# Latent attention in ascending tiles, with keys and queries made in one stream between the attention's half steps

## The chip, the cores and the metric

The kernel runs on one core of one Trainium2 chip. The metric is the device time of one execution in microseconds. Five engines work side by side, each with an in-order instruction queue: TensorE (PE, matrix products and transposes, results in PSUM), VectorE (DVE), ScalarE (ACT), GpSimd (POOL) and SyncE (SP, which here only starts DMA transfers).

## The reference

A trunk of two layers on a sequence of 1024 tokens with 1024 features, all float32. A layer normalises its input, projects it once, and feeds four branches of 256 features each: A (gated causal depthwise convolution of 31 taps, LayerNorm, swish, pointwise product), B (HGRN2, a gated linear recurrence), C (Mamba-2 SSD in chunks) and D (multi-head latent attention). The outputs are gated, concatenated, projected with `w_out`, normalised and added to the input. What changes is mostly branch D:

```python
def mla_branch(cq, ckv, k_rope, gate, positions, qa_g, qb_w, kva_g, kvb_w):
    q = (rms_norm(cq, qa_g) @ qb_w).reshape(bsz, s, D_HEADS, D_NOPE + D_ROPE)
    q = jnp.concatenate([q[..., :D_NOPE], apply_rotary(q[..., D_NOPE:], positions)], axis=-1)
    kv = (rms_norm(ckv, kva_g) @ kvb_w).reshape(bsz, s, D_HEADS, D_NOPE + D_VDIM)
    ...
    mask = key_chunk[None, :] <= q_chunk[:, None]
    p = jax.nn.softmax(jnp.where(mask, sc, MASK_VALUE), axis=-1)
    return (p @ v) * jax.nn.silu(gate)
```

It has 4 heads, a query rank of 256, a key/value rank of 128, 64 plain and 32 rotary features a head and 64 value features. The mask is causal by chunks of 64 tokens, so a tile of 128 queries reads the keys of its own tile and of all tiles before it.

## The kernel before, in words

Work goes by tiles of 128 tokens (`NT` = 8) and, where features lie in the partitions, by halves of 512 tokens. The normalised input stands transposed in SBUF as two pools of 32 KB a partition, a high and a low part (`hT`), because large projections are made of three products of split operands. The output weights, split in the same way by `th_w` (L939), take the place of `hT`: they can be written when the last projection has read it.

Each branch is a set of Python generators ("threads"): `th_conv` (L470, the 31 taps on DVE, 30 multiply-adds of 128x512 for each of 2 feature halves and 2 sequence halves), `th_atail` (L482, LayerNorm, swish and product of branch A for the two sequence halves), `th_b`, `th_x` and `th_c` (L715, the scan of branch C, tile by tile), `gate_f` (gates of A and D), `th_d` (L788, the latents of D), `th_q` (L852, queries of D), `th_att` (L883, attention), `th_w` and `th_o` (L987, the first output tile). `PLAN` (L44) gives each thread a start, an end and a total of work units, and `weave` (L259) always runs the thread whose position in that plan is earliest. So the plan sets the order in which instructions are written down; a scheduler then orders them for each engine by when they could start, with the written order as priority, and gives out the buffers.

In `th_d`, for each tile of `ORDER` (L37, 7 down to 0): 24 products into `psd` (L206 to L208), copies `cn` and `krd` out of it, the squares and `rstd_p` on POOL (L143, L144), the query scale `rq` on DVE, transposes of `cn` (L823), copies `ckT` and `cqT`; then `pk` (L832), the scaled keys `kk` and values `vD`, the rotary part of the key (five DVE operations), transposes of the keys (L845) and copies `kT`. Keys of all tiles stay in `kT`, query latents in `cqT`. `th_q` makes the queries of a tile from `cqT`: `pq` (L857), scaled copy, four rotary operations on DVE, transposes `ptq` (L870), copy `qTt`. Rows 96 to 99 of `kT` and `qTt` hold mask factors that DMAs on POOL's queue bring.

`th_att` goes through `ORDER` too. For each pair of heads (`m`) it makes the scores of two heads (`psc`, L900), their negated maximum (`nm`, L903, DVE), the exponentials with their sums (`pe`, L905, ACT), yields, then transposes the exponentials (`ptp`, L914), copies them (`pT`, three of four on DVE) and multiplies with the values (`poD`, L918). A tile ends with the reciprocal of the sums spread over 256 columns on DVE (`rsD`, L925), its two transposes (`prsD`, L928) and two multiplications with the gate `gD`. Attention of tile 7 comes first and needs the keys of all tiles, so attention begins when `th_d` has ended. `th_o` multiplies the first output tile (`ORDER[0]`) by the output weights; the other tiles follow in the same order, and so does the next layer.

PSUM has two tiles of two banks (`big`: `psd`, `pk`, `psc`, `pz` and others) and two single banks for each of two groups (`sm`): one group holds `ptp`, `ptA` and others, the other `ptx`, `pcb`, `pyC` of branch C and `pq`, `ptq`, `poD` of D. In SBUF the groups of buffers that matter are `t1k` (six of 256 columns: `xdt`, `xsd`, `btk`, `yo` of branch C, `gD`, `rsD`, `yD` of D) and `blk` (19 of 512 columns).

Of the kernel before, what the change touches and what calls it, by code (L numbers as in the profile page):

```python
# [15 lines left out]
ALU = mybir.AluOpType  # L16
# [8 lines left out]
NT1, NT15, NT2 = 6, 2, 4  # L25
# [11 lines left out]
ORDER = list(range(NT))[::-1]  # L37
# [35 lines left out]
    "gd1": (261.8, 280.6, 21),  # L73
    "x1": (212.9, 255.7, 61.5),
    "at1": (278.6, 342, 22),
    "c1": (275.5, 340.6, 48.2),
    "d1": (266.1, 351.4, 72),
    "q1": (335.5, 349.5, 2),
    "o1": (479.4, 508.2, 8.2),
    "att1": (347.1, 481.6, 144.8),  # L80
# [16 lines left out]
def trunk_kernel(ctx, tc, x, pos, pre_g, post_g, wd, wv, w256, wo, cols, rows, pw, qb, kvb,  # L97
# [161 lines left out]
    def weave(threads, until):  # L259

        while threads:
            t = min(threads, key=Thread.pos)
            if t.pos() > until:
                return
# [11 lines left out]
    for l in range(L):  # L276
# [193 lines left out]
        def th_conv():  # L470
            for m in range(2):
                w = [col[:, C_DWW + m * 31 + k:C_DWW + m * 31 + k + 1] for k in range(31)]
                for h in range(2):
# [8 lines left out]
        def th_atail():  # L482
            for g in range(2):
# [231 lines left out]
        def th_c():  # L715
            hst = small(256, "hst", 1)
            G.memset(hst, 0.0)
            for g4 in range(2):
                gt = get_gate(2, g4)
                ms = small(8, "msc", 2)  # L720
                for j in range(4):
# [51 lines left out]
                    jk = br.tile([P, 256], BF16, tag="jk", name="jkC", bufs=1)  # L773
# [11 lines left out]
        kT, vD, cqT = {}, {}, {}  # L785
        rq = small(NT, "rq", 1)

        def th_d():  # L788
# [7 lines left out]
            for i in ORDER:  # L796
                g = i // 4
                if (0, g) not in kT:
                    for h in range(4):
                        kT[h, g] = blk("kT", parts=100)  # L800

                        nc.gpsimd.dma_start(out=kT[h, g][96:100, :], in_=amask[0])
                    for c in range(2):
                        cqT[c, g] = blk("cqT")
# [7 lines left out]
                ms = small(2, "msd", 3)  # L812
# [3 lines left out]
                krd = small(32, "krd", 2, (P, 2, 16))  # L816
                copy("krd", krd.rearrange("p a j -> p (a j)"), ps[:, 384:416])
                A.activation(jd[:, 0:256], cn[:, 0:256], AF.Square, scale=1.0 / 16, accum_out=ms[:, 0:1])
                A.activation(jd[:, 256:384], cn[:, 256:384], AF.Square, scale=128.0 ** -0.5, accum_out=ms[:, 1:2])
                rstd_p(ms, ms)  # L820
                V.tensor_scalar(rq[:, i:i + 1], ms[:, 0:1], SCALE, None, op0=ALU.mult)
# [15 lines left out]
                k1, k2 = small(32, "kr1", 2, (P, 2, 16)), small(32, "kr2", 2, (P, 2, 16))  # L837
                V.tensor_tensor(k1, krd, cosT[:, i], op=ALU.mult)
                for a in range(2):
                    V.tensor_tensor(k2[:, a, :], krd[:, 1 - a, :], sinT[:, i, a, :], op=ALU.mult)  # L840
                V.tensor_tensor(k1, k1, k2, op=ALU.add)
                V.tensor_copy(kk[:, :, 64:96],
                              k1.rearrange("p a j -> p (a j)").unsqueeze(1).to_broadcast([P, 4, 32]))
# [4 lines left out]
                yield 3  # L848

        qTs = {}  # L850

        def th_q():  # L852
            for i in ORDER:
                csl = slice((i % 4) * P, (i % 4 + 1) * P)
                pq = sm("pq")
                for c in range(2):
                    T.matmul(pq[:, 0:384], cqT[c, i // 4][:, csl], qbt[:, c, :], start=(c == 0), stop=(c == 1))  # L857
                qk = tmp(384, "qk", (P, 4, 96))
                scaled("qk", qk.rearrange("p h d -> p (h d)"), pq[:, 0:384], rq[:, i:i + 1])
                t1, t2 = small(128, "rt1", 1, (P, 4, 2, 16)), small(128, "rt2", 1, (P, 4, 2, 16))  # L860
                qr = qk[:, :, 64:96].rearrange("p h (a j) -> p h a j", a=2)
                V.tensor_tensor(t1, qr, cosT[:, i].unsqueeze(1).to_broadcast([P, 4, 2, 16]), op=ALU.mult)
                for a in range(2):
                    V.tensor_tensor(t2[:, :, a, :], qr[:, :, 1 - a, :],
                                    sinT[:, i, a, :].unsqueeze(1).to_broadcast([P, 4, 16]), op=ALU.mult)
                V.tensor_tensor(qk[:, :, 64:96], t1.rearrange("p h a j -> p h (a j)"),
                                t2.rearrange("p h a j -> p h (a j)"), op=ALU.add)
# [3 lines left out]
                qTt = br.tile([100, 4, P], F32, tag="qTt", name="qTt", bufs=2)  # L871
                nc.gpsimd.dma_start(out=qTt[96:100, :, :].rearrange("p h t -> p (h t)"), in_=amask[1 + i % 4])
                copy("qTt", qTt[0:96, :, :].rearrange("p h t -> p (h t)"), ptq[0:96, :])
                qTs[i] = qTt
                yield 1

        q_steps = th_q()

        def th_q0():
            yield next(q_steps)  # L880
            yield next(q_steps)

        def th_att():  # L883
            for i in ORDER:
# [273 lines left out]
```

## Time and profile before

| | us |
|---|---|
| median of 3 runs (1263.44 to 1266.04) | 1265.05 |
| the profiled execution | 1263.62 |
| its span | 1261.8 |
| PE busy | 1195.5 |
| DVE busy | 876.9 |
| ACT busy | 445.3 |
| POOL busy | 184.2 |

The profile is of one execution; its time is 1.8 us more than the span from the first to the last instruction. Busy time of PE is time in which at least one product is under way by the profiler's model; time of an engine that is not busy is idle. Layer 0 takes about the first 640 us, layer 1 the rest. In each layer the convolution ends some 350 us (in layer 1 at about 968) into the span, the latents of D some 90 us later, and attention about 545 (1162); the output projection follows.

### The profile page before, as it was taken

The page shows a single profiled execution, that of the slowest core. Times are in us where ns is not written, and L with a number is a line of the kernel's source. Part 1 is how long each engine was busy: PE and PEld are TensorE (multiplying, and loading weights), DVE is VectorE, ACT ScalarE, POOL GpSimd, SP SyncE. Part 2 cuts the span into 40 slices and gives each one's busy share as a digit, 9 for nine tenths or more (in the row PEclk, how much of TensorE's full clock was granted, in tenths as well). Part 3 has the DMA queues.
Part 4 walks back from the last instruction along what each step waited for, and adds up shares of the span by engine and source line. Part 5 has one row for each costly group of instructions (what it writes and reads, how often), then busy time and mean ns, then how long its engine had stood idle before and what let it go on. Part 6 is the DMA issues. An engine that isn't in the chain of part 4 may idle for free.

```text
span 1261.8 us, 17893 instructions
## 1 busy us (share of the span) xinstructions
PE 1195.5 (95%) x6902; PEld 985.5 (78%) x6902; DVE 876.9 (69%) x1687; ACT 445.3 (35%) x1028; POOL 184.2 (15%) x290
## 2 busy tenths in 40 slices
PE   5999999899989989999999999998999998999997
PEld 5988998888878746678888889887888776566886
DVE  5564699999876386745453839999997763867232
ACT  5412222222374364434332222221225644644211
POOL 2100020111033111111020001211012322112000
PEclk9999999999999999999999999999999899999999
DMA  7102122111151040144321111211013311202531
GB/s 274 34 34 68 43 76 85 67 46 51 55 165 60 22 152 24 56 154 137 114 97 60 41 50 59 84 63 64 34 62 124 105 35 55 93 18 68 188 128 72
DMA packets 38660, 101.47 MB, mean 80 GB/s; under 512 B 5440, under 2 KB 13808, under 8 KB 38576
## 3 DMA queue, kind: packets, MB, share of 16 engines
q1 hardware_dynamic: 22848, 51.42, 12.0%
q0 software_dynamic: 14864, 46.04, 11.0%
q10 hardware_dynamic: 864, 2.88, 0.6%
q8 instruction: 54, 0.88, 0.3%
q14 instruction: 30, 0.25, 0.1%
HBM read 75.37 MB, written 25.20 MB: 80 GB/s over the span
## 4 chain that ended last, share of the span: by engine, by line
PE 40%; DVE 11%; ACT 2%; issue 1%; DMA 1%; POOL 0%; DVEq 0%; ACTq 0%
PE pz L982 11%; DVE ca L478 2%; PE psx L217 2%; PE psx L223 2%; PE psx L220 2%; DVE amat L639 2%; PE psc L900 1%; DVE qz L632 1%; PE psA L217 1%; PE psA L220 1%; PE psA L223 1%; PE poD L918 1%; PE ptp L914 1%; PE psd L206 1%; PE psd L208 1%
## 5 line engine op out<-in xcount | busy, mean ns | idle before, releaser
L478 DVE SCALAR_TENSOR_TENSOR ca<-hpad,col,ca 128x512 f32<-128x512 f32 x240 | 179.8, 751 | 3.6
L173 DVE TENSOR_TENSOR wl<-raw,wh 128x1024 fp32r<-128x1024 f32 (+2 forms) x56 | 66.9, 1194 | 81.0 <-ACT wh L157 80.9
L157 ACT CAST wh<-raw 128x1024 fp32r<-128x1024 f32 (+2 forms) x56 | 57.5, 1028 | 154.0 <-PE psA L220 33.7
L982 PE MATMUL pz<-woh,yh 128*128 128x512 f32 x240 | 77.8, 403 | 0.2 <-ACT yh L157 0.2
L982 PE MATMUL pz<-woh,yl 128*128 128x512 f32 x240 | 75.6, 396 | 0.0
L982 PE MATMUL pz<-wol,yh 128*128 128x512 f32 x240 | 75.4, 396 | 0.0
L206 PE MATMUL psg<-wh,hh 128*128 128x256 f32 x256 | 74.4, 291 | 1.1 <-DVE amat L608 1.1
L622 PE MATMUL plB<-qz,krb 128*128 128x128 f32 x448 | 63.6, 287 | 10.8 <-DVE krb L633 10.6
L900 PE MATMUL psc<-kT,qTt 96*128 96x512 f32 (+4 forms) x192 | 72.6, 501 | 1.2 <-ACT pe L905 1.1
L208 PE MATMUL psg<-wh,hl 128*128 128x256 f32 x256 | 73.1, 286 | 0.0
L207 PE MATMUL psg<-wl,hh 128*128 128x256 f32 x256 | 72.7, 284 | 0.0
L905 ACT ACTIVATE pe<-psc,nm 128x1024 f32<-128x1024 f32 (+7 forms) x64 | 47.3, 739 | 63.5 <-DVE nm L903 63.0
L622 PEld LDWEIGHTS plB<-qz,krb 128*128 128x128 f32 x448 | 57.0, 197 | 13.6 <-issue 7.1
L217 PE MATMUL psx<-hh,wh 128*128 128x512 f32 x192 | 62.8, 404 | 0.0
L223 PE MATMUL psx<-hh,wl 128*128 128x512 f32 x192 | 62.0, 399 | 0.0
L220 PE MATMUL psx<-hl,wh 128*128 128x512 f32 x192 | 61.2, 400 | 0.0
L173 DVE TENSOR_TENSOR yl<-yt,yh 128x512 fp32r<-128x512 f32 x16 | 11.0, 690 | 65.2 <-ACT yh L157 65.2
L982 PEld LDWEIGHTS pz<-woh,yl 128*128 128x128 f32 x240 | 45.3, 189 | 10.5 <-issue 0.2
L982 PEld LDWEIGHTS pz<-wol,yh 128*128 128x128 f32 x240 | 45.3, 189 | 10.5
L903 DVE TENSOR_REDUCE nm<-psc 128x1 f32<-128x1024 f32 (+7 forms) x64 | 47.1, 744 | 9.0 <-PE psc L900 9.0
L914 PE MATMUL ptp<-idn,pe 128*128 128x128 f32 x288 | 46.8, 282 | 6.0 <-ACT pe L905 5.8
L157 DVE COPY pT<-ptp 128x512 f32<-128x512 f32 (+3 forms) x72 | 38.0, 546 | 20.5 <-PE ptp L914 20.4
(331 smaller groups left out, 3076.0 us busy)
## 6 DMA issues: line engine op xcount, KB each, us to landing
raw<-in_w_dram SPq DMA_DIRECT2D x44, 512.0 KB, 3.5
rawo<-in_wo_dram SPq DMA_DIRECT2D x16, 512.0 KB, 4.3
gsp<-gt POOLq DMA_DIRECT2D x16, 256.0 KB, 2.6
gl<-gsp POOLq DMA_DIRECT2D x8, 512.0 KB, 5.5
gspF<-gtA POOLq DMA_DIRECT2D x16, 256.0 KB, 2.3
ysp<-gl POOLq DMA_DIRECT2D x8, 512.0 KB, 3.4
lm<-acsp POOLq DMA_DIRECT2D x16, 256.0 KB, 4.1
yt<-ysp SPq DMA_DIRECT2D x16, 256.0 KB, 3.4
```

Source lines behind the costliest of these rows:

```text
L157: (V.tensor_copy if name in ONV else A.copy)(out_, in_)
L173: V.tensor_tensor(lo, src, hi.bitcast(F32), op=ALU.subtract)
L206: T.matmul(ps[:, :n], a, hs[k], start=(k == 0), stop=False)
L207: T.matmul(ps[:, :n], a, ls[k], start=False, stop=False)
L208: T.matmul(ps[:, :n], b, hs[k], start=False, stop=(k == KD - 1))
L217: T.matmul(ps[:, h * 512:(h + 1) * 512], w, hh[:, k, h * 512:(h + 1) * 512], start=(k == 0), stop=False)
L220: T.matmul(ps[:, h * 512:(h + 1) * 512], w, hl[:, k, h * 512:(h + 1) * 512], start=False, stop=False)
L223: T.matmul(ps[:, h * 512:(h + 1) * 512], wl, hh[:, k, h * 512:(h + 1) * 512], start=False, stop=(k == KD - 1))
L478: V.scalar_tensor_tensor(t, hp[:, k:k + 512], w[k], t, op0=ALU.mult, op1=ALU.add)
L622: T.matmul(pl[:, o0:o0 + P].rearrange("p (r b u) -> p r b u", r=2, u=u), k_[:, t_ * P:(t_ + 1) * P], z[:, :, t_ * P:(t_ + 1) * P].rearrang ...
L900: T.matmul(psc[:, c0:c1_], qTt[0:k_, h, :], kT[h, c0 // 512][0:k_, 0:c1_ - c0], start=True, stop=True)
L982: T.matmul(pz[n], a[:, k, :], w[:, k, n * 512:(n + 1) * 512], start=(k == 0 and a is yh and w is wh), stop=(k == KD - 1 and a is yl))
```

## The change

`ORDER` is ascending. `th_d` and `th_q` become one generator, `th_kq`, that makes keys, values and queries of one tile in four steps; `th_att` first runs it for two tiles (`AHEAD`), and then takes one step of it after each of the four half steps of an attention tile, so that tile i+2 is made during tile i and the last one during tile 5. The query latent is no longer stored for all tiles (`cqT`), and the rotary part of key and queries of a tile is made together (five heads, five DVE operations). The query scale moves to POOL. For tiles 0 to 3 the scores of two heads share one PSUM tile and one maximum. The reciprocal is taken of the four sums, and POOL spreads it over 256 columns; its transposes go into the upper half of the bank of `poD`. The masks and the gate of D are loaded on SP's queue; `gD` has one buffer of its own, and `t1k` has five. The convolution goes by sequence half, the two halves of branch A's tail are threads of their own (the first planned at 236 instead of 296), and the gate of D is planned about 10 units earlier. The place of `hT` is given to the output weights when `th_kq` has written down the last tile's projection.

```diff
-NT1, NT15, NT2 = 6, 2, 4
+NT1, NT15, NT2 = 5, 2, 4
-ORDER = list(range(NT))[::-1]
+ORDER = list(range(NT))
+AHEAD = 2
-    "gd0": (278.8, 298.3, 21),
+    "gd0": (268, 287, 21),
-    "at0": (296.3, 363.8, 22),
+    "at00": (236, 262, 11),
+    "at10": (302, 340, 11),
-    "d0": (283.6, 373.2, 72),
-    "q0": (357.3, 375.6, 2),
-    "att0": (347.7, 481.2, 144.8),
+    "att0": (288, 481.2, 217.6),
...
-        while threads:
+        while threads and not until():
...
         def th_conv():
-            for m in range(2):
-                for h in range(2):
+            for h in range(2):
+                for m in range(2):
...
-        def th_atail():
-            for g in range(2):
+        def th_atail(g):
...
+        def th_kq():
...
-                        nc.gpsimd.dma_start(out=kT[h, g][96:100, :], in_=amask[0])
-                    for c in range(2):
-                        cqT[c, g] = blk("cqT")
+                        nc.sync.dma_start(out=kT[h, g][96:100, :], in_=amask[0])
...
                 proj_tok(hT, hs, ls, i, ND, ps)
+                made.append(i)
...
+                rp = tmp(160, "rp", (P, 5, 2, 16))
+                copy("krd", rp[:, 4, :, :].rearrange("p a j -> p (a j)"), ps[:, 384:416])
...
-                V.tensor_scalar(rq[:, i:i + 1], ms[:, 0:1], SCALE, None, op0=ALU.mult)
+                G.tensor_scalar(ms[:, 2:3], ms[:, 0:1], SCALE, None, op0=ALU.mult)
+                yield 2.25
...
-                for c in range(2):
-                    copy(f"cqT{c}", cqT[c, g][:, csl], pt[:, c * P:(c + 1) * P])
-                yield 6
+                cqt = tmp(256, "cqt")
+                copy("cqt", cqt, pt[:, 0:256])
+                yield 2.25
                 pk_ = big("pk")
                 T.matmul(pk, ckT, kvt, start=True, stop=True)
+                pq = sm("pq")
+                for c in range(2):
+                    T.matmul(pq[:, 0:384], cqt[:, c * P:(c + 1) * P], qbt[:, c, :], start=(c == 0), stop=(c == 1))
...
+                scaled("qk", rp[:, 0:4, :, :].rearrange("p h a j -> p h (a j)"), pqv[:, :, 64:96], ms[:, 2:3])
+                scaled("qk", qk[:, :, 0:64], pqv[:, :, 0:64], ms[:, 2:3])
+                V.tensor_tensor(t1, rp, cosT[:, i].unsqueeze(1).to_broadcast([P, 5, 2, 16]), op=ALU.mult)
...
+                yield 2.25
                 for h in range(4):
                     T.transpose(ptk[0:96, h * P:(h + 1) * P], kk[:, h, :], idn)
...
+                qTt = br.tile([100, 4, P], F32, tag="qTt", name="qTt", bufs=AHEAD + 1)
+                nc.sync.dma_start(out=qTt[96:100, :, :].rearrange("p h t -> p (h t)"), in_=amask[1 + i % 4])
...
         def th_att():
+            kq = th_kq()
+            for _ in range(4 * AHEAD):
+                yield next(kq)
             for i in ORDER:
...
-                po = sm("poD")[:, 0:256]
+                pob = sm("poD")
+                po, prs = pob[:, 0:256], pob[:, 256:512]
-                gt = tmp(256, "gD", (P, 2, P))
-                nc.gpsimd.dma_start(out=gt, in_=feat(gspF, 1, i * P, (i + 1) * P))
+                gt = small(256, "gD", 1, (P, 2, P))
+                nc.sync.dma_start(out=gt, in_=feat(gspF, 1, i * P, (i + 1) * P))
...
                     yield i + 1
+                    w = next(kq, None)
+                    if w is not None:
+                        yield w
...
+                V.reciprocal(sume, sume)
                 rs = tmp(256, "rsD", (P, 4, 64))
-                V.reciprocal(rs, sume.unsqueeze(2).to_broadcast([P, 4, 64]))
-                prs = sm("prsD")[:, 0:256]
+                G.tensor_copy(rs, sume.unsqueeze(2).to_broadcast([P, 4, 64]))
...
-        weave(ths, plan("d")[1] + 0.5)
+        weave(ths, lambda: len(made) == NT)
         hpool.release()
```

## Rows read from the trace of the kernel before

**Rows 1.** the page, part 1, the whole span: busy us (share), instructions

```profile
PE 1195.5 (95%) x6902; PEld 985.5 (78%) x6902; DVE 876.9 (69%) x1687; ACT 445.3 (35%) x1028; POOL 184.2 (15%) x290
```

**Rows 2.** busy by stretch: us, PE, PEld, DVE, ACT, POOL busy (instructions), granted clock

```profile
140.00:350.00 210.00, 205.08 (x1277) 181.04 (x1277) 200.14 (x354) 51.19 (x90) 31.05 (x44) 0.98 0.19 63
350.00:444.00 94.00, 86.19 (x504) 72.52 (x502) 56.88 (x191) 50.28 (x165) 24.48 (x41) 1.00 0.24 79
444.00:457.00 13.00, 8.10 (x24) 4.14 (x24) 9.98 (x18) 9.14 (x22) 5.15 (x5) 0.87 0.56 177
457.00:480.00 23.00, 21.92 (x142) 13.63 (x141) 19.09 (x25) 15.35 (x24) 2.38 (x5) 1.00 0.34 116
480.00:533.00 53.00, 51.52 (x393) 35.37 (x392) 38.39 (x77) 22.49 (x55) 9.31 (x14) 1.00 0.09 28
533.00:545.00 12.00, 9.77 (x64) 7.03 (x63) 9.98 (x21) 5.28 (x16) 2.23 (x4) 0.86 0.39 116
760.00:968.00 208.00, 201.09 (x1257) 176.44 (x1257) 196.31 (x341) 50.18 (x88) 30.21 (x42) 0.99 0.18 63
968.00:1064.00 96.00, 89.11 (x504) 75.45 (x503) 56.22 (x185) 49.99 (x165) 24.17 (x40) 0.96 0.24 78
1064.00:1081.00 17.00, 11.34 (x37) 5.41 (x36) 12.71 (x26) 12.99 (x28) 5.15 (x5) 0.90 0.46 154
1081.00:1150.00 69.00, 67.32 (x499) 45.39 (x499) 52.30 (x92) 32.55 (x67) 9.71 (x15) 1.00 0.12 37
1150.00:1162.00 12.00, 10.21 (x80) 7.03 (x75) 9.66 (x24) 6.72 (x23) 2.86 (x4) 1.00 0.38 118
```

**Rows 3.** timeline of PE, 444 to 480: start, length, line, operation, idle before

```profile
445.69 1.12 PE L832 MATMUL pk<-kvt,ckT 128*128 128x512 f32 x2 [1.67 <-DVE ckT L157]
449.13 0.80 PE L845 MATMUL pk<-idn,kk 128*96 128x128 f32 x4 [2.32 <-ACT vD L163]
...
450.58 4.75 PE L900 MATMUL psc<-kT,qTt 96*128 96x512 f32 x8
...
465.17 1.67 PE L900 MATMUL psc<-kT,qTt 96*128 96x512 f32 x4
```

**Rows 4.** groups on DVE by shape, 340 to 560: busy us, mean ns, idle

```profile
L925 DVE RECIPROCAL rsD<-sume 128x256 f32<-128x256 f32 x8 | 13.9, 1742 | 0.0
...
L491 DVE BATCH_NORM_STATS2 stA<-ptA 128x6 f32<-128x256 f32 x8 | 3.4, 423 | 0.0
...
L513 DVE SCALAR_TENSOR_TENSOR glA<-pyA,col,glA 128x512 f32<-128x512 f32 x4 | 3.0, 748 | 0.7 <-PE pyA L512 0.7
...
L864 DVE TENSOR_TENSOR rt<-qk,sinT 128x64 f32<-128x64 f32 x16 | 2.9, 217 | 0.0
...
L497 DVE TENSOR_SCALAR hnA<-hnA,mvA 128x256 f32<-128x256 f32 x8 | 2.7, 405 | 0.5 <-POOL mvA L144 0.5
```

**Rows 5.** waits of PE, whole span: total us, times, longest

```profile
PE prsD L928 <- DVE rsD L925: 1.7, 2, 1.2
```

**Rows 6.** groups on POOL by shape, whole span

```profile
L647 POOL TENSOR_TENSOR qp<-qz 128x512 f32<-128x512 f32 x8 | 12.3, 1542 | 21.6 <-DVE qz L632 21.6
...
L891 POOL DMA_DIRECT2D gD<-gspF x16 | 11.5, 721 | 2.0 <-issue 2.0
```

**Rows 7.** timeline of POOL, 445 to 450 us

```profile
445.59 1.83 POOL L143 TENSOR_TENSOR msd<-msd,eps 128x2 f32<-128x2 f32 x1 [10.04 <-ACT jd L819]
...
448.19 0.19 POOL L143 TENSOR_TENSOR msc<-msc,eps 128x8 f32<-128x8 f32 x1
```

**Rows 8.** timeline of DVE, 444 to 449 us

```profile
445.55 1.21 DVE L173 TENSOR_TENSOR wol<-rawo,woh 128x1024 fp32r<-128x1024 f32 x1
```

**Rows 9.** waits of SP's queue, whole span: total us, times, longest

```profile
SPq L943 <- DVE ckT L157: 174.3, 2, 88.2
```

**Rows 10.** timeline of PE, line 733 (first step of a branch C tile)

```profile
382.01 0.60 PE L733 MATMUL ptx<-idn,xbc 128*128 128x128 f32 x4
...
412.87 0.60 PE L733 MATMUL ptx<-idn,xbc 128*128 128x128 f32 x4
```

More of the change, by code (lines that the diff above doesn't have):

```diff
@@ L470, in th_conv @@
         def th_conv():
-            for m in range(2):
-                w = [col[:, C_DWW + m * 31 + k:C_DWW + m * 31 + k + 1] for k in range(31)]
-                for h in range(2):
+            for h in range(2):
+                for m in range(2):
+                    w = [col[:, C_DWW + m * 31 + k:C_DWW + m * 31 + k + 1] for k in range(31)]
                     hp = hpads[m, h]
@@ L772, in th_c @@
                     V.tensor_tensor(gt[:, j, :], xsf, gt[:, j, :], op=ALU.mult)
-                    jk = br.tile([P, 256], BF16, tag="jk", name="jkC", bufs=1)
+                    jk = br.tile([P, 384], BF16, tag="jd", name="jkC", bufs=1)
                     for g in range(2):
@@ L782, in th_c @@
                 yield 0.1
-        kT, vD, cqT = {}, {}, {}
-        rq = small(NT, "rq", 1)
-        def th_d():
+        kT, vD, qTs = {}, {}, {}
+        made = []
+        def th_kq():
             nc.gpsimd.dma_start(out=qbt, in_=qb[l])
@@ L811, in th_d @@
                 proj_tok(hT, hs, ls, i, ND, ps)
-                ms = small(2, "msd", 3)
+                made.append(i)
+                ms = small(3, "msd", 3)
                 cn = tmp(384, "cn")
@@ L847, in th_d @@
                     copy(f"kT{h}", kT[h, g][0:96, csl], ptk[0:96, h * P:(h + 1) * P])
[L848 to L867, printed above, removed]
                 ptq = sm("ptq")
@@ L893, in th_att @@
                     pes = []
-                    for r in range(2):
-                        h = 2 * m + r
-                        psc = big("psc")
-                        for c0 in range(0, n, 512):
-                            c1_ = min(n, c0 + 512)
-                            k_ = 100 if c1_ == n else 96
-                            T.matmul(psc[:, c0:c1_], qTt[0:k_, h, :], kT[h, c0 // 512][0:k_, 0:c1_ - c0],
-                                     start=True, stop=True)
-                        nm = small(1, "nm", 3)
-                        V.tensor_reduce(nm, psc[:, 0:n], AX.X, ALU.max, negate=True)
-                        pe = k4("pe")
-                        A.activation(pe[:, 0:n], psc[:, 0:n], AF.Exp, bias=nm, accum_out=sume[:, h:h + 1])
-                        pes.append(pe)
+                    nm = small(2, "nm", 3)
@@ new lines, in th_att @@
+                    if i < 4:
+                        psc = big("psc")
+                        pe = k4("pe", (P, 2, 512))
+                        for r in range(2):
+                            T.matmul(psc[:, r * 512:r * 512 + n], qTt[:, 2 * m + r, :], kT[2 * m + r, 0][:, 0:n],
+                                     start=True, stop=True)
+                        pv = psc.rearrange("p (r k) -> p r k", r=2)[:, :, 0:n]
+                        V.tensor_reduce(nm, pv, AX.X, ALU.max, negate=True)
+                        scs = [psc[:, r * 512:r * 512 + n] for r in range(2)]
+                        pes = [pe[:, r, 0:n] for r in range(2)]
+                    else:
+                        scs = []
+                        for r in range(2):
+                            psc = big("psc")
+                            for c0 in range(0, n, 512):
+                                c1_ = min(n, c0 + 512)
+                                k_ = 100 if c1_ == n else 96
+                                T.matmul(psc[:, c0:c1_], qTt[0:k_, 2 * m + r, :], kT[2 * m + r, c0 // 512][0:k_, 0:c1_ - c0],
+                                         start=True, stop=True)
+                            V.tensor_reduce(nm[:, r:r + 1], psc[:, 0:n], AX.X, ALU.max, negate=True)
+                            scs.append(psc[:, 0:n])
+                            pes.append(k4("pe")[:, 0:n])
@@ L920, in th_att @@
                                  for j in range(j0, j1) for r in (1, 0))
-                    if m == 1:
-                        next(q_steps, None)
                     yield i + 1
+                    w = next(kq, None)
+                    if w is not None:
+                        yield w
+                V.reciprocal(sume, sume)
                 rs = tmp(256, "rsD", (P, 4, 64))
-                V.reciprocal(rs, sume.unsqueeze(2).to_broadcast([P, 4, 64]))
-                prs = sm("prsD")[:, 0:256]
+                G.tensor_copy(rs, sume.unsqueeze(2).to_broadcast([P, 4, 64]))
                 for m in range(2):
@@ L1007, in trunk_kernel @@
         wo_t["l"] = wpool.tile([P, KD, D], F32R, name=f"wol{l}")
-        ths += [Thread(th_att(), *plan("att")), Thread(th_w(), *plan("w")), Thread(th_o(), *plan("o"))]
-        weave(ths, 1e9)
+        ths += [Thread(th_w(), *plan("w")), Thread(th_o(), *plan("o"))]
+        weave(ths, lambda: False)
         br.release()
```

45 lines of the change are left out of this document (19 added, 26 removed).

## The prediction

> **What bounds the kernel now.** I read the page's part 1 first: TensorE is busy 1195.5 us, 95% of the span of 1261.8, and the next engine, DVE, 69% [rows 1]. So the whole kernel holds 66.3 us in which TensorE (PE) stands idle. A change that leaves PE's products as they are, as this one does, can win only there and where PE runs at its lower clock.
>
> The second view is the busy time by stretch [rows 2]. Idle of PE is a stretch's length less PE's busy time. From 140 to 350 (HGRN2, the convolution, the projections of branch C) two engines are full at once, PE with 205.08 of 210 us and DVE with 200.14. From 350 to 444 branch C's scan, branch A's tail and the latents of branch D share the chip: 7.81 us idle. From 444 to 457, between the last latents and the first attention, 4.90 of 13 us, at a mean granted clock of 0.87. The attention proper, 457 to 533, has 1.08 + 1.48 = 2.56, and its last, short tiles, 533 to 545, have 2.23. The five parts of layer 1 read 6.91, 6.89, 5.66, 1.68 and 1.79 in the same way. What lies after the convolution, and so within reach of this change, is 17.50 in layer 0 and 16.02 in layer 1: 33.5 us.
>
> The third view, PE's timeline at the dense hole, says why it is there [rows 3]. PE waits 1.67 us for ckT of the last tile made and 2.32 us before the transposes of its keys. Tiles go down from 7, and attention of tile 7 reads the keys of all eight, so the chain of the last tile (projection, norm, keys, scores) has nothing beside it. Behind the hole PE runs for a while at the lower of its two clock levels, 1.2 instead of 2.4 GHz: eight score products take 4.75 us where four take 1.67 later, so 4.75 - 2 x 1.67 = 1.4 us are lost a layer.
>
> **The change, part by part.** PE's work: the same products and transposes are issued, in another order, so nothing there is saved.
>
> The hole. Ascending, with keys and queries of tile i+2 made between the half steps of tile i, the last tile's chain has attention of tile 5 beside it. I take the hole away in full: 4.90 + 5.66 idle and 2 x 1.4 for the clock, **-13.4**. The bounds are 0 (it moves) and that.
>
> The stretch before it, 7.81 + 6.89 = 14.7 idle. Waits of branch C and of the latents now have attention products beside them, but the first two tiles of keys are made before any attention, so a new fill stands at its head. Bounds 0 and -14.7. I take a third, **-5**, nearer the lower end because PE is 92% busy there already.
>
> The end of attention, 2.23 + 1.79 = 4.0 idle. The last tile is now the widest, with long products and the first output projection behind it; the short tiles move to where other work covers them. Bounds -4.0 and, if a wide tile's chain is as bare, +4.0; I take **-1.5**.
>
> DVE. The reciprocal of 256 columns, 1.742 us a tile, becomes one of four columns, between 0 and 1.742, taken at the 0.217 of the smallest operation shown [rows 4]. Nine rotary operations become five that are a little wider, and the query scale and one copy leave: six operations at about 0.217. That is 1.5 + 1.3 = 2.8 us a tile, 45 us in all, but DVE is busy only 56.88 of 94 and 57.48 of 76 us after the convolution [rows 2], and PE waited for that reciprocal 1.7 us in the whole run [rows 5]. This I count in the end of attention, and nothing more. ScalarE gets one more piece a tile and one wider copy; with 50.28 of 94 us busy it hides them.
>
> GpSimd (POOL). The broadcast that the reciprocal did becomes a POOL copy of 128x256, and the query scale a one-column POOL operation. POOL showed no such copy. It lies between the 0.19 of a tiny addition [rows 7] and the 1.542 of an addition with two inputs and twice the columns [rows 6]; I take 0.8, half of the latter. So reciprocal and copy take 1.0 where 1.74 stood, but the PE transposes of the sums are queued in order behind it, and whatever PE work is placed behind those waits too. Bounds -1.7 (the wait goes) and 16 x 1.54 = +25; I take **+1**, since the old, longer step made PE wait only twice.
>
> One row speaks against that step. The same POOL addition took 1.83 us at 445.59 and 0.19 a moment later [rows 7], and at 445.55 DVE had begun a 1.21 us subtraction with two inputs [rows 8]. The Trainium skill (SBUF - State Buffer, Who interferes with whom) says that VectorE and GpSimd share a port pair as an exclusive lock, so that the later one waits for the whole of the other's instruction. The 1.83 agrees with it. By that rule each of the 16 new copies could wait for such a subtraction or hold one up, which would be an estimate of some 16 x 1.6 = 26 us on POOL, of which PE would see only those that stand beside the weight splits, three tiles a layer; by the row alone the term stays +1.
>
> DMAs. 48 issues leave POOL's queue for SP's: sixteen key masks, sixteen query masks, sixteen gate loads, the last at 0.721 us each [rows 6]. POOL is not late, so nothing is won. On SP they stand among the output weight loads, and a load of those once stood 88.2 us at the head of that queue, until the last projection freed the place of its destination [rows 9]. What would be late then is the mask of tile 7 and the gates of tiles 6 and 7, but the projection that frees the place now comes in tile 5, and the gates are needed only at a tile's end. I take 0; without that cover a landing each would show.
>
> Branch A. The convolution goes by halves of the sequence, and the first half of A's tail moves forward into the full stretch: half of 3.4 + 2.7 + 3.0 us of DVE [rows 4], 4.55 a layer, where DVE has 10 of 210 us left. The gate projection of D moves forward as well, which takes a plain PE filler from the end. Bounds 0 and 4.55 a layer; PE has its own backlog there, so I take 1 each, **+2**.
>
> The output weights. Their eight splits (1.21 us of DVE each [rows 8], as much again on ScalarE) now fall on tiles 5 to 7. In 457 to 480 half of them stood beside wide attention tiles and PE lost 1.08 of 23 us [rows 2]. All eight there: 1 more a layer, **+2**, bounds 0 and 9.7 a layer (all of DVE's part bare).
>
> Sum: -13.4 - 5 - 1.5 + 1 + 2 + 2 = -14.9. The profiled execution took 1263.62 us (1.8 around its span); less 14.9 that is 1248.7. It stands 1.4 below the median of 1265.05, so the prediction is **1250**.
>
> **The rivals.** *Slower: the small PSUM buffers.* The output of an attention tile (poD) holds one of the two buffers that branch C (ptx, pcb, pyC) and the new stream (pq, ptq) also need, from its first product to the gate; when the next tile takes the second, both are gone for at least reciprocal and copy, 1.0 us. Before, attention began when C was done. C's tiles came every (412.87 - 382.01) / 3 = 10.3 us [rows 10], and PE was 92% busy, so there is slack, but little; one short buffer less (five for six) adds to it. If each of 16 C tiles loses 1.1 us that PE can't fill, that is +18, and the -5 falls away: -14.9 + 5 + 18 = +8, **1273**. It decides from about (14.9 - 5) / 16 = 0.6 us a tile. Against it: late tiles of C hold up nothing before the output projection, and attention can run meanwhile.
>
> *No change: the hole only moves.* The order on an engine is not the plan's: the weight load is planned late in the attention and yet stood 88.2 us in SP's queue [rows 9]. If the interleaving is not kept, the fill of the first two tiles or the weight splits make a hole of the old size: -14.9 + 13.4 = -1.5, **1263.5**. Against it: keys of tile 7 are no longer a condition for the first scores, whatever the order.
>
> *Much faster.* The stretch before the hole closes too (-14.7 for -5), the end of attention as well, and the added terms stay at +1: -13.4 - 14.7 - 3 + 1 = -30, **1235**. For it: every chain there is one of latencies, and DVE gets 45 us lighter.
>
> **How the numbers follow.** The forecast has 0.52 and a range of its own of 1241 to 1259; much faster 0.13, no change 0.13, slower 0.22. Two tenths of a per cent, 2.5 us, is about what a measurement can tell from no change. So faster is 0.52 + 0.13 = 0.65, same 0.13, slower 0.22. The range, 1233 to 1272, takes in the no-change case, most of the fast one and the lower half of the slow one.
>
> **What would show it.** Right: no wait over 1 us of PE before the first wide scores, full clock there, PE idle from the convolution's end to the output projection at some 10 us a layer, DVE near 830 us. The old hole is wrong if PE waits for ckT or vD with no other product between. The slow rival shows as waits of ptx, pcb or pq for a release by yD or pyC; the POOL term as waits of prs for rsD. The whole is wrong if idle falls and the time does not.

## The result, and the profile after

The changed kernel takes **1313.39 us** (median of 4 runs, 1308.65 to 1319.36) where the kernel before took 1264.41 beside it: ratio 1.039, 95% interval 1.0364 to 1.0417. Forecast was 1250, with a range that ended at 1272. The profiled execution took 1319.36 us, its span is 1317.6, so 55.8 us are to be found between the two traces.

The page of the changed kernel, the span and part 1, answers to [rows 1]:

```profile
span 1317.6 us, 17860 instructions
...
PE 1217.2 (92%) x6902; PEld 996.3 (76%) x6902; DVE 850.8 (65%) x1575; ACT 445.4 (34%) x1040; POOL 168.0 (13%) x274
```

PE's products are the same 6902. It is busy 1217.2 - 1195.5 = 21.7 us longer with them, and idle 100.4 us instead of 66.3, so 34.1 longer. Where, is read from four stretches: from the end of the convolution to the last output product of layer 0, to the first convolution step of layer 1, to the end of that convolution, and to the end. Busy times of the kernel before (length, PE, PEld, DVE, ACT, POOL, granted clock, the DMAs' share, GB/s):

```profile
345.00:642.00 297.00, 278.95 (x1597) 215.87 (x1596) 178.19 (x378) 141.40 (x366) 55.18 (x88) 0.99 0.30 97
642.00:692.00 50.00, 49.76 (x313) 44.35 (x312) 23.80 (x53) 16.08 (x39) 8.13 (x16) 1.00 0.21 72
692.00:963.00 271.00, 264.09 (x1543) 227.86 (x1542) 238.30 (x415) 63.62 (x108) 29.14 (x40) 0.99 0.17 59
963.00:1262.00 299.00, 275.65 (x1547) 212.07 (x1545) 162.98 (x362) 123.93 (x330) 49.74 (x78) 0.98 0.27 89
```

The same four stretches of the changed kernel:

```profile
348.00:660.00 312.00, 280.39 (x1543) 215.02 (x1542) 160.70 (x308) 139.35 (x367) 43.99 (x80) 0.95 0.27 88
660.00:717.00 57.00, 56.76 (x345) 50.08 (x344) 24.94 (x55) 17.99 (x43) 7.41 (x15) 1.00 0.21 73
717.00:994.00 277.00, 269.56 (x1569) 231.16 (x1568) 241.90 (x427) 64.59 (x109) 30.80 (x41) 0.99 0.18 61
994.00:1318.00 324.00, 281.33 (x1522) 214.68 (x1520) 146.03 (x293) 123.57 (x334) 40.26 (x71) 0.95 0.24 80
```

The first and the last lose 15 and 25 us, and there alone the granted clock falls, from 0.99 and 0.98 to 0.95. That is an estimate of a tenth of the stretch at 1.2 GHz, half of the full clock, where it was two to four hundredths. Idle time in them grows from 18.05 to 31.61 and from 23.35 to 42.67, 32.9 of the 34.1 us. So the loss sits where branch C's scan, the key and query stream and attention stand beside each other, and behind that. From the end of the convolution to the first output product alone PE is idle 27.1 and 32.8 us (348 to 556 and 994 to 1208.5), where it was 17.5 and 16.0 (345 to 542.5 and 963.5 to 1161.5).

Waits of PE in the changed kernel (total us, times, longest), those that the text speaks of:

```profile
PE pyC L748 <- DVE lm L742: 8.2, 7, 2.6
PE pty L967 <- DMA yt<-ysp: 6.9, 2, 4.5
PE psc L899 <- ACT pe L905: 4.6, 4, 2.1
...
PE pcb L741 <- ACT btk L157: 3.7, 3, 2.2
PE pyC L748 <- DVE rp L157: 3.4, 2, 2.3
PE psd L206 <- ACT pe L905: 3.2, 4, 1.5
...
PE ptx L730 <- ACT qTt L157: 3.0, 2, 2.3
...
PE pk L830 <- DVE ckT L157: 2.2, 5, 0.7
...
PE pq L833 <- DVE lm L742: 2.2, 1, 2.2
...
PE ptx L730 <- DVE yD L935: 1.1, 1, 1.1
...
PE pyC L748 <- ACT qk L163: 0.9, 1, 0.9
...
PE pyC L748 <- ACT qTt L157: 0.7, 1, 0.7
...
PE ptx L730 <- ACT qk L163: 0.4, 1, 0.4
PE poD L920 <- DVE xsd L768: 0.4, 1, 0.4
...
PE ptq L858 <- ACT btk L157: 0.3, 1, 0.3
...
PE pq L833 <- DVE xsd L768: 0.2, 1, 0.2
```

Read them with the code at hand. `pcb` is made of `xbc` alone and needs nothing of `btk`; what it waits for is that the copy `btk` has read `ptx`, whose bank it takes. `qk` reads `pq`, `qTt` reads `ptq`, `lm` (L742) reads `pcb`, `yD` reads `poD`, `xsd` (L768) reads `pyC`. So ten of these rows are waits for a bank of the pair that C and the stream share, 12.9 us together. The other rows are something else. `ckT` is an input of `pk`, and `yt` one of `pty`. `pyC` needs `lm`, and its row for `rp` belongs to `lm` too: that `rp` is copied out of `psd`, a large tile, and at 1059.9, the longer of its two places, `lm` ended at 1059.71, `rp` at 1059.81, and `pyC` began at 1059.86. In the kernel before, two rows are waits for a bank of that pair:

```profile
PE pcb L744 <- ACT btk L157: 3.4, 2, 1.7
...
PE prsD L928 <- ACT qTt L157: 0.4, 2, 0.2
```

`psc` and `psd` need nothing of `pe`, which reads an earlier `psc`: those are waits for the other PSUM pair, that of the large tiles. With `pk` (1.6) and the `psc` of L886 (1.2) they are 10.6 us, where the kernel before has 1.1.

The timeline of PE in the changed kernel, 413 to 442 us, with the small PSUM tiles of one pair alone:

```profile
413.32 0.69 PE L920 MATMUL poD<-pT,vD 128*64 128x128 f32 x2
413.94 1.12 PE L730 MATMUL ptx<-idn,xbc 128*128 128x128 f32 x4
...
418.43 0.61 PE L741 MATMUL pcb<-xbc,xbc 128*128 128x128 f32 x4
420.24 1.10 PE L748 MATMUL pyC<-xdt,lm 128*128 128x64 f32 x8 [1.20 <-DVE lm L742]
...
424.35 1.46 PE L833 MATMUL pq<-qbt,cqt 128*128 128x384 f32 x4
...
431.29 0.60 PE L858 MATMUL ptq<-idn,qk 128*96 128x128 f32 x4
...
436.04 0.60 PE L730 MATMUL ptx<-idn,xbc 128*128 128x128 f32 x4
438.84 0.71 PE L741 MATMUL pcb<-xbc,xbc 128*128 128x128 f32 x4 [2.20 <-ACT btk L157]
```

And the readers that set those banks free, on DVE and ScalarE in the same stretch:

```profile
416.63 0.36 ACT L157 COPY btk<-ptx 128x256 f32<-128x256 f32 x1
...
423.74 0.42 DVE L768 TENSOR_TENSOR xsd<-pyC,xsd 128x256 f32<-128x256 f32 x1
...
426.17 0.47 ACT L163 ACTIVATE qk<-pq,msd 128x256 f32<-128x256 f32 x1
...
433.03 0.58 ACT L157 COPY qTt<-ptq 96x512 f32<-96x512 f32 x1
...
440.65 0.42 DVE L935 TENSOR_TENSOR yD<-poD,gD 128x256 f32<-128x256 f32 x1
```

`poD` holds its bank from 413.32 to 441.07, 27.7 us, and ptx, pcb, pyC, pq, ptq and the next ptx go through the other bank one at a time: pyC is last read until 424.16 and pq begins at 424.35. That bank is not taken all the time: ptq is read until 433.61, and ptx begins at 436.04, behind other products in PE's order. C's tiles follow each other at 413.94 and 436.04, 22.1 us; from the first (369.79) to the eighth (477.20) it is 15.3 us a tile, where [rows 10] has 10.3.

### The profile page after: what moved, and what is told of

It reads as the page before. It is cut to its first block, busy times and chain, and to the rows that moved or that the text cites. A ratio compares the mean times of both kernels' runs of the same rounds, so it can differ in the third digit from the quotient of the medians.

```text
span 1317.6 us, 17860 instructions
## 1 busy us (share of the span) xinstructions
PE 1217.2 (92%) x6902; PEld 996.3 (76%) x6902; DVE 850.8 (65%) x1575; ACT 445.4 (34%) x1040; POOL 168.0 (13%) x274
## 5 line engine op out<-in xcount | busy, mean ns | idle before, releaser
L905 ACT ACTIVATE pe<-psc,nm 128x128 f32<-128x128 f32 (+7 forms) x64 | 47.2, 739 | 36.0 <-DVE nm L901 27.9
L899 PE MATMUL psc<-kT,qTt 96*128 96x512 f32 (+4 forms) x128 | 53.3, 543 | 4.7 <-ACT pe L905 4.6
L985 PEld LDWEIGHTS pz<-wol,yh 128*128 128x128 f32 x240 | 45.8, 191 | 10.6
L916 PEld LDWEIGHTS ptp<-idn,pe 128*128 128x128 f32 x288 | 36.1, 148 | 21.8 <-issue 8.5
L985 PEld LDWEIGHTS pz<-woh,yh 128*128 128x128 f32 x240 | 45.0, 192 | 9.4
```

The lines of the kernel that those rows point to most:

```text
L899: T.matmul(psc[:, c0:c1_], qTt[0:k_, 2 * m + r, :], kT[2 * m + r, c0 // 512][0:k_, 0:c1_ - c0], start=True, stop=True)
L916: T.transpose(ptp[:, (j - j0) * P:(j - j0 + 1) * P], pes[r][:, j * P:(j + 1) * P], idn)
L985: T.matmul(pz[n], a[:, k, :], w[:, k, n * 512:(n + 1) * 512], start=(k == 0 and a is yh and w is wh), stop=(k == KD - 1 and a is yl))
```

## The experiments

Three questions, in this order: which part of the change costs the time, with what it collides, and by which resource. All ratios are to the kernel before on the same chip, its median there between 1262 and 1264 us.

**Ascending order alone**, in the kernel before:

```diff
-ORDER = list(range(NT))[::-1]
+ORDER = list(range(NT))
```

> The kernel before with one change: tiles go up instead of down; latents of all tiles are still made in their own thread and attention is planned after it. Theory 1 (branch C's chain and the stream's chain wait for each other once attention runs beside C): the order alone leaves attention planned behind C, so the time stays between 1255 and 1275 us, with PE idle in C's stretch of 6 to 12 us a layer. Rival (the ascending order itself costs, because the last tile is the widest and the output projection starts with tile 0): 1280 or more, with the new idle at the end of attention.

1270.97 us, ratio 1.0057 (1.0041 to 1.0072). The order costs some 7 us. The hole before attention stays: 440 to 460 has PE busy 14.75 of 20 us at a granted clock of 0.74.

**Branch A's part undone** in the changed kernel (convolution by feature half, both halves of the tail and the gate of D at their old places in the plan):

```diff
-    "at00": (236, 262, 11),
-    "at10": (302, 340, 11),
+    "at00": (296.3, 330, 11),
+    "at10": (330, 363.8, 11),
...
-            for h in range(2):
-                for m in range(2):
+            for m in range(2):
+                for h in range(2):
```

> The changed kernel with branch A's part undone: convolution by feature halves, the two halves of A's tail planned where the one thread was, the gate of D planned where it was. Theory 1: that part is worth at most the 4.6 us of DVE a layer and the gate as filler, so 1300 to 1315. Rival (the plain filler of the gate projection and the early half tail are what C's stretch lacks): 1285 or less, with PE idle in C's stretch back under 12 us a layer.

1319.58, ratio 1.0439 (1.0401 to 1.0478). Not the cause: undoing it gains nothing, and by the medians it is worth 6 us to the changed kernel, though the two intervals still touch.

**The short end of a tile alone**, in the kernel before:

```diff
-                po = sm("poD")[:, 0:256]
+                pob = sm("poD")
+                po, prs = pob[:, 0:256], pob[:, 256:512]
...
-                V.reciprocal(rs, sume.unsqueeze(2).to_broadcast([P, 4, 64]))
-                prs = sm("prsD")[:, 0:256]
+                V.reciprocal(sume, sume)
+                G.tensor_copy(rs, sume.unsqueeze(2).to_broadcast([P, 4, 64]))
```

> The kernel before with only the end of an attention tile changed: reciprocal of four sums on DVE, the spread over 256 columns as a POOL copy, the transposes in the bank of poD. Theory 1 and my term for it: 1261 to 1267, DVE some 24 us less busy (16 tiles of 1.5 us). Rival (the POOL copy in the chain of each tile makes PE wait): 1270 or more, with waits of prs for rsD above 10 us in all.

**1257.67**, ratio 0.9956 (0.9936 to 0.9976): faster than both kernels, and the shortest of this study that computes all of the trunk. DVE is busy 856.4 for 876.9.

**The short end and branch A's part**, in the kernel before (both diffs above, forwards):

> The kernel before with the short end of the attention tile and branch A's part of the change (convolution by sequence halves, the first half tail early, the gate of D planned earlier), tiles still going down. In the changed kernel branch A's part was worth 6 us. If that holds without the stream: 1249 to 1254. If it only helped because the stream had lost its cover: 1255 to 1260, no different from the short end alone.

1273.04, ratio 1.0081. Branch A's part costs 15 us here, and nothing in the changed kernel. What it does hangs on what stands beside it; why, was not tried.

**The masks and gates back on POOL's queue**, in the changed kernel:

```diff
-                        nc.sync.dma_start(out=kT[h, g][96:100, :], in_=amask[0])
+                        nc.gpsimd.dma_start(out=kT[h, g][96:100, :], in_=amask[0])
...
-                nc.sync.dma_start(out=gt, in_=feat(gspF, 1, i * P, (i + 1) * P))
+                nc.gpsimd.dma_start(out=gt, in_=feat(gspF, 1, i * P, (i + 1) * P))
```

> The changed kernel with the masks and the gate of D loaded on POOL's queue again. If SP's queue is the cause (a mask or a gate stands behind another wait there, and attention waits for it): 1290 or less. Theory 1: 1305 to 1320.

1315.05, ratio 1.0417: the queue is not the cause.

**Both kernels without branch C's scan** (what th_c computes is left out, and its place in the plan kept by one yield):

```diff
-                for j in range(4):
...
-                yield 0.1
+                yield 24.1
```

> The kernel before without branch C's scan: the gate of C is loaded and written out unmultiplied, nothing else of the scan runs (its products, exponentials and additions are left out; the projections and short convolutions of C stay). It is the base of the next run. PE loses about 25 us of C's products a layer, so both theories expect 1195 to 1230 us.

> The changed kernel without branch C's scan, left out in the same way. Theory 1 (attention and the stream lose because C's chain stands beside them on the same queues): within 10 us of the kernel before without C, so the loss of 49 us is mostly gone. Rival (the stream dealt between the half steps is slow by itself, its steps and the attention's wait for each other): 30 us or more above the kernel before without C, with waits of psd, psc and pk for pe in the stretch after the convolution.

The kernel before falls to 1225.32 (ratio 0.9706), the changed one to 1217.97 (0.9648). Without the scan the change wins 7.4 us; with it, it loses 49. So the stream itself is sound, and the whole loss is what it and branch C do to each other.

**Is it C's decay matrices?** `lm` is loaded, masked and exponentiated per tile of C, in a group of four buffers that it shares with `pT` and, since the change, `qk`. In the kernel before its exponentials end 2 to 52 us ahead of its product with `xdt`, most for the last tile of a layer; in the changed one 1 to 20 us ahead, and the costliest wait of a C product is `pyC` for `lm`. First the lead is taken from the kernel before:

```diff
-NT1, NT15, NT2 = 6, 2, 4
+NT1, NT15, NT2 = 6, 2, 3
...
-                    lm = tmp(512, "lm", (P, 4, P))
+                    lm = shaped(br.tile([P, 512], F32, tag="lm", name="lm", bufs=1), (P, 4, P))
```

> The kernel before with one buffer of its own for branch C's decay matrices lm (in place of the four that it shared with the attention's pT; that pool gets three, so the memory is the same). This takes away the lead with which the kernel before makes them (its last lm transfer lands some 50 us before its last use) and nothing of the order of the work. Theory 1, that the changed kernel loses its time because lm comes just in time in each tile of C (load, add and exp in series): at least +25 us, so 1288 us or more. Rival, that lm's buffers are not what sets C's pace: at most +8 us, so 1256 to 1272.

Then two buffers of its own are given to it in the changed kernel, at the price of one 4 KB buffer, and that price is taken alone:

```diff
-NK4 = 7
+NK4 = 6
...
-                    lm = tmp(512, "lm", (P, 4, P))
+                    lm = shaped(br.tile([P, 512], F32, tag="lm", name="lm", bufs=2), (P, 4, P))
```

> The changed kernel with two buffers of their own for lm, so that its transfer no longer waits for a turn among pT and qk; paid for with one of the seven 4 KB buffers. Theory 1 (lm's lead): at most 1290 us, the wait of GpSimd's load on poD gone. Rival (the one-bank PSUM pairs, or in-order queues): 1305 us or more.

> Control for the run with lm's own buffers: the changed kernel with six in place of seven 4 KB buffers and nothing else. Both theories: 1310 to 1325 us.

1288.81 (1.0209, 1.0182 to 1.0236), 1329.61 (1.0527) and 1318.13 (1.0423). The lead is worth 26 us to the kernel before, as the theory asked. (The edit takes a buffer from `pT` too, but attention does not feel it: from the first scores to the last it takes 86.8 and 87.0 us for 86.3 and 87.3.) And yet giving `lm` buffers in the changed kernel repairs nothing: its exponentials then end 20 us or more ahead in every tile, PE waits for it 4.5 us in place of 8.4, and the time is 11 us above the run with the price alone. The theory falls as the cause: its first half was a true cost in the wrong kernel.

**Is it the small PSUM banks?** A first try moved C's three tiles into the other pair and `ptp` in beside `poD`:

```diff
-SMA = ("psgA", "psg", "ptp", "psV", "ptA", "pt2A", "pyA", "pstC", "dsB", "pzA", "pty")
+SMA = ("psgA", "psg", "ptx", "pcb", "pyC", "psV", "ptA", "pt2A", "pyA", "pstC", "dsB", "pzA", "pty")
```

> The changed kernel with ptx, pcb and pyC of branch C moved to the other pair of single PSUM banks, and ptp to the pair of poD, pq and ptq, so that C never waits for a bank of branch D. If the small banks are the cause (the slower rival of the prediction): 1290 or less, and the waits of ptx and pyC for qTt, qk and yD are gone with a C tile every 11 us instead of 15. Theory 1 (the chains meet on the in-order engines, not in the banks): 1300 to 1325, a C tile still every 14 us or more.

1335.7, ratio 1.0564. I took that as evidence against the banks. The waits of PE say otherwise:

```profile
PE poD L920 <- DVE pT L157: 15.2, 15, 2.5
...
PE ptp L916 <- DVE pT L157: 11.6, 12, 2.8
```

The transposes `ptp` now share a pair with `poD`, so they go one at a time: the shortage was moved to another tile, not lifted. Counted from the end of the convolution, C's last product ends 20 and 14 us earlier than in the changed kernel, and attention's 11 and 12 us later. The costliest row there is another, `pty` for `yt`, 23.0 us in four places, all behind that late end. Next, all four banks as one group:

```diff
-        tag = "smA" if name in SMA else "smB"
-        return psm.tile([P, 512], F32, tag=tag, name=name)
+        return psm.tile([P, 512], F32, tag="sm", name=name, bufs=4)
```

> The changed kernel with its four one-bank PSUM buffers as one group of four that any of the tiles may take, in place of two fixed pairs. Rival (poD holds a bank that C's ptx, pcb, pyC and the stream's pq need): 1295 us or less. Theory 1 (lm's lead): 1305 us or more.

1312.2, ratio 1.0385, which speaks against the banks again, until the time is split by stage. That kernel:

```profile
0.00:362.00 362.00, 336.92 (x1936) 290.72 (x1937) 279.23 (x496) 100.59 (x189) 43.13 (x67) 0.98 0.22 75
362.00:657.00 295.00, 277.87 (x1565) 215.08 (x1564) 160.25 (x309) 139.66 (x370) 44.94 (x81) 0.98 0.29 95
657.00:714.00 57.00, 52.49 (x317) 47.38 (x316) 23.41 (x52) 17.20 (x39) 6.89 (x14) 0.94 0.19 63
714.00:1007.00 293.00, 274.09 (x1544) 234.47 (x1543) 240.29 (x423) 61.41 (x105) 30.01 (x40) 0.95 0.17 56
1007.00:1312.00 305.00, 277.77 (x1547) 213.82 (x1546) 147.28 (x298) 125.45 (x337) 39.84 (x72) 0.98 0.26 86
```

The stretches with C and attention take 295 and 305 us, 17 and 19 less than in the changed kernel; those before, with HGRN2 and the convolution, take 362 for 348 and 293 for 277. A gain of 36 us and a loss of 30 stood in one number. So the group of four was given to the time of the stream and attention alone, the smallest move was tried beside it, and the kernel before got the same group:

```diff
+    def banks(four):
+        psm[0].release()
+        psm[:] = [tc.alloc_tile_pool(name="psm", bufs=4 if four else 2, space=PSUM), four]
...
         def th_att():
+            banks(1)
...
         weave(ths, lambda: False)
+        banks(0)
```

> The changed kernel; from the beginning of th_att to the end of the layer's attention the four one-bank PSUM buffers are one group, before and after that two pairs as they were. Theory 2 (poD holds one bank of its pair through a whole attention tile, so C's ptx, pcb, pyC and the stream's pq, ptq take turns in the other): the stretch from the convolution to the end of attention shrinks as in the run with one group throughout, by 25.6 + 21.1 = 47 us, without the loss before it: 1265 to 1280 us. Theory 3 (the chains of C, of the short attention tiles and of the latents simply have too little plain work beside them, whatever the buffers): 1300 us or more.

```diff
-SMA = ("psgA", "psg", "ptp", "psV", "ptA", "pt2A", "pyA", "pstC", "dsB", "pzA", "pty")
+SMA = ("psgA", "psg", "ptp", "psV", "ptA", "pt2A", "pyA", "pstC", "dsB", "pzA", "pty", "ptx", "pcb")
```

> The changed kernel with two of branch C's tiles, ptx and pcb, in the pair of ptp, and nothing else. Theory 2: the crowded pair is relieved of two of its six users, and the other has been given two; between 1275 and 1300 us. Theory 3: 1305 to 1325 us.

> The kernel before with the same one group of four from the beginning of th_d on. Theory 2: attention begins there when C has ended, so poD takes nothing from C, and the time stays within 8 us of 1263. If it falls by more than 8 us, the group of four is a gain of its own, and the repair of the changed kernel by it says less about the overlap.

**1274.94** (1.0097, 1.0078 to 1.0116), 1298.96 (1.0284, 1.0255 to 1.0312) and 1280.8 (1.0144, 1.012 to 1.0168). The group of four takes 38.5 us off the changed kernel, the move of two tiles 14.4, both as the banks would have it. That the pair is short is shown by these runs; that `poD` is what makes it so is read from the timeline, as no run moved `poD` alone. (The expectation counted to the end of attention; the changed kernel's last attention tile already has output products beside it, so the longer stretches here are the fairer account.) It is no gain of its own: the kernel before, where attention begins when C has ended, gets 18 us slower by it, so it is not neutral there, as I had expected within 8 us, but what it wins in the changed kernel it wins there alone. Its waits name poD for pT (8.6 us) and ptq for qk (5.6); what makes it slower was not settled. The stretches of the repaired kernel:

```profile
349.00:646.00 297.00, 277.02 (x1572) 214.26 (x1571) 160.13 (x309) 140.06 (x371) 44.74 (x81) 0.99 0.29 95
646.00:696.00 50.00, 49.76 (x315) 44.40 (x314) 23.07 (x52) 16.54 (x39) 6.84 (x14) 1.00 0.22 72
696.00:972.00 276.00, 269.07 (x1560) 231.20 (x1559) 241.60 (x427) 63.27 (x107) 30.86 (x41) 0.99 0.18 61
972.00:1274.00 302.00, 272.74 (x1532) 210.20 (x1530) 145.38 (x295) 125.09 (x336) 39.15 (x71) 0.98 0.26 86
```

297, 50, 276 and 302 us against 297, 50, 271 and 299 of the kernel before; the clock is back at 0.99 and 0.98. And in its timeline of PE three of the tiles that took turns now stand together, while poD holds the fourth bank (ptx is read until 423.67):

```profile
420.03 0.64 PE L862 MATMUL ptq<-idn,qk 128*96 128x128 f32 x4
420.51 0.60 PE L734 MATMUL ptx<-idn,xbc 128*128 128x128 f32 x4
421.04 0.66 PE L925 MATMUL poD<-pT,vD 128*64 128x128 f32 x8
421.63 0.71 PE L745 MATMUL pcb<-xbc,xbc 128*128 128x128 f32 x4
```

**The last 12 us.** In the repaired kernel PE waits for lm about as long as in the changed one (8.2, and 3.4 under the name of `rp`), and longer than in the kernel before (2.5):

```profile
PE pyC L752 <- DVE lm L746: 10.7, 8, 3.0
```

So lm was written down one tile ahead of its use, and, in a second kernel, attention was planned later:

```diff
-                    lm = tmp(512, "lm", (P, 4, P))
...
+                    if i < NT - 1:
+                        lms[i + 1] = decay(i + 1)
+                    lm = lms[i]
```

> The changed kernel with the group of four banks from attention's begin, and branch C's decay matrix lm written down one tile ahead of its use. If lm, which PE still waits for 10.7 us there (2.5 in the kernel before), is what is left: 1262 to 1269 us. If not: 1272 us or more.

```diff
-    "att0": (288, 481.2, 217.6),
+    "att0": (303, 481.2, 217.6),
...
-    "att1": (272, 481.6, 217.6),
+    "att1": (287, 481.6, 217.6),
```

> The changed kernel with the group of four banks from attention's begin, and the attention stream planned 15 units later in both layers. If what is left comes from C and the short attention tiles standing beside each other: 1262 to 1270 us. If that overlap is harmless once the banks are one group: 1272 us or more, since the work that covers the late tiles is moved away.

1267.53 (1.0043, 1.0026 to 1.0059) and 1274.42 (1.0103). With the banks free, lm is the next bound, 7.4 us, and its wait is down to 2.7; planning attention later gains nothing. What is left, 4 us, is less than ascending order cost by itself in the kernel before, and was not followed. Two candidates have no run: the pair of large tiles, whose waits for `pe` are still 7.0 us in the repaired kernel and 5.0 in the one with `lm` ahead, and the buffer that `t1k` lost.

## Why the prediction was wrong, point by point

**The step that failed** is the second term: "The stretch before it ... I take a third, -5", with bounds of 0 and -14.7. The term that excluded a loss measured +26 us of idle time up to the first output product (59.9 for 33.5, where I expected some 10 a layer) and +33 with the output projection. Most of the +22 busy stands there too: in the first and the last stretch a product takes 0.182 and 0.185 us of PE for 0.175 and 0.178, an estimate of some 10 us in each. The mechanism stood among the rivals, as the slow one, and was told there as it is: poD holds one of two banks that ptx, pcb, pyC, pq and ptq need. It was sized wrongly. I priced the moment in which both banks are gone, 1.0 us for reciprocal and copy, 1.1 a tile of C, +18 and 1273. But poD holds its bank from its first product to the gate, 14 to 28 us in the tiles that stand beside C, and for all of that five others, ptx, pcb, pyC, pq and ptq, queue through one bank. The group of four gives 38.5 / 16 = 2.4 us a tile of C back. That attention can run meanwhile, which I set against it, does not hold: pq and ptq, which feed attention, stand in the same queue. That the C products that waited were also the filler of the short attention tiles is my reading, and no run separates it.

Its mark was only half right: waits for a release were there, 12.9 us against 3.8, but less than a quarter of the 55.8, and of those by yD or pyC, which I had named, only 1.3 of ptx and pq; most were releases by btk, qTt and lm. The rest came as longer waits of other kinds and as the lower clock. Of these waits, the repaired kernel has lost `pty` for `yt` (6.9), and part of those of the large tiles for `pe` (10.6, now 7.0) and of `poD` for `pT` (7.0, now 3.6); how the banks lengthen them, by products placed later in PE's order with nothing beside them, is argued. The Trainium skill (Perfetto Trace Analysis, Optimization Strategy) says that a gap which repeats on the engine that should be full can mean that there is not enough PSUM for the next tile. Here the sign was weaker than that: ten different rows for the small pair, the largest 3.7 us.

**The hole**, -13.4: right in its mechanism; its size was not measured by itself. pk waits for ckT 2.2 us (6.1 before), and the wait for vD, 4.7 before, is gone. That ascending order alone keeps it shows that the stream removes it. Its share of the lower clock was not won, since PE fell to 1.2 GHz elsewhere.

**The end of attention**, -1.5: PE is busy 24.00 of the 24 us from 556. But a stall that I did not list stands behind it, pty for yt, 6.9 us in two places; it is gone in the repaired kernel.

**DVE**: on no path, as said, but 26 us lighter and not 45. The reciprocal takes 0.172 us (0.217 taken). The short end alone takes 20.5 us of busy time off DVE (856.4 for 876.9), so the other edits, the rotary ones among them, come to 5.6, where 16 x 1.3 = 21 were forecast.

**POOL's copy**: 0.41 us where I took 0.8. The end of a tile taken alone won 5 us, so this edit was worth more than its +1.

**DMAs**, 0: right. But the 88.2 us of [rows 9] ended with the split `wol` (444.11 to 445.33), which reads the buffer that the next load writes: the load itself waited for that buffer, not for the place of the weights. **Branch A**, +2: no cost in the changed kernel (-6 by the medians), and +15 in the kernel before. **Output weights**, +2: not told apart.

**The sum**: without C's scan, where the banks are not short, the change gives -7.4. The forecast had the right sign for that part, and twice the size; what stood beside it in the kernel decided.

## What to carry to other kernels

Before two chains are put side by side, list the buffers that both take turns in and how long the slowest holder keeps one; a holder that lives through a whole tile turns a pair into a single buffer, and the price is that of every user behind it, not that of the moment in which none is free. Where an order is planned, a short buffer shows as lateness spread over many waits more than as one wait for its release, so split the time by stage: a repair that loses elsewhere, as the group of four did, reads as no effect in the total. And a cost shown in one kernel, as lm's lead was, is no evidence that it bounds the other.

## What the runs showed of the hardware

The POOL copy of 128x256 has a median of 0.408 us and once took 1.39. POOL and DVE in the changed kernel at that place:

```profile
1130.36 1.39 POOL L929 COPY rsD<-sume 128x256 f32<-128x256 f32 x1
```

```profile
1130.27 1.22 DVE L777 TENSOR_TENSOR gl<-gl,msc 128x1024 f32<-128x1024 f32 x1 [1.77 <-POOL msc L144]
```

It ended 0.26 us after a DVE multiplication with two inputs that had begun 0.09 before it. The Trainium skill (SBUF — State Buffer, Who interferes with whom) has it that the two engines lock each other out of a shared port pair; this one of 16 agrees, the other 15 took at most 0.46, and PE lists no wait for this copy. Three of the 15 began 0.10 us into a two-input addition of 0.29 us, and took 0.45. In the run of the short end alone, a copy that began 0.11 us into `yl` from `yt` and `yh` (0.68 us, both inputs in SBUF) took 0.83 us and ended 0.26 after it; one that began 0.27 us into `yl` from `pty` and `yh` (0.69 us, one input in PSUM) took 0.41 and ended before it.
